# V projection of a hybrid decoder layer: the seventh chunk of its first pass formed by seven block products instead of eight

## The chip, the cores and the metric

One core of one Trainium2 chip runs the whole layer. The metric is device time in microseconds (us). A difference of 0.2% of this kernel's time, 2.2 us, is about what a measurement of it can tell from no change.

## The reference

One decoder layer for 256 tokens, 2048 features wide, in float32. One projection gives queries, keys and values of two groups of eight heads; differential attention in one group, block-sparse attention in the other; an output projection; layer norm; a gated feed-forward with a short convolution; layer norm again. What the change touches is the value columns of the first line below:

```
proj = h @ w_in[l]
v_d = proj[..., 2048:3072]        # 1024 value columns, differential heads
v_m = proj[..., 5120:6144]        # 1024 value columns, block-sparse heads
a_out = diff_attention(q_d, k_d, v_d, ...)
b_out = moba_attention(q_m, k_m, v_m, ...)
mix = concatenate([a_out, b_out]) @ w_out[l]
```

## The kernel before, in words

**Products.** Every float32 operand is split into a rounded part `hi` and a rest `lo` that TensorE (PE) takes in its faster format, and a product of two operands is three matmuls: hi·hi, hi·lo, lo·hi. ScalarE (ACT) writes `hi` by a copy, VectorE (DVE) writes `lo` as a difference.

**V projection.** It stands first in the program, as 16 chunks of the weight stream (`stream`, lines 80 to 84), numbered 0 to 15 here and in the code's `i`. Chunks 0 to 7 are the first pass and give value columns 0 to 1023, chunks 8 to 15 the second pass, columns 1024 to 2047. A chunk is 256 rows by 1024 columns of the weight, four blocks of 128x512. The step of a chunk (`run_v`, line 961) adds its share to four PSUM banks: bank 0 to 3 for token half t and column half c, as `CB[t][c]`, so that c = 1 is banks 1 and 3. An ordinary step is 24 matmuls of 128x512 (`mm_pair`), c = 0 first, then c = 1. Both passes use the same four banks, so the second pass may start on a bank only when ACT has copied the first pass's result out of it (`v_copy`): c = 0 in the middle of step 7, c = 1 at the beginning of step 8.

**Steps by seven products.** Chunks 9, 12 and 15 (`SEVEN`, line 51) go by a Strassen-like form: seven products of sums of blocks, 21 matmuls (`mm_seven`, line 737). Its operands are four sums of activation blocks (`act_sums`, DVE; `act_sums_split`, ACT and DVE), four sums of weight blocks and three raw weight blocks. They lie in the tiles `vhi` and `vlo` of seven blocks: places 0 to 2 are the raw blocks, 3 to 6 the sums. The tiles exist once, so a chunk's parts can be written only when the chunk by seven before it is done. `blocks_raw` (line 647) writes the raw blocks' hi by ACT, their lo by a negated ACT copy and an accumulating DMA on GpSimd's queue (POOL), and the first two sums; `blocks_lo`, `blocks_sum` and `blocks_hi` do the other two sums one after the other, since each is made from the one before, in the same buffer. Four of the seven products need partner sums that go to banks 4 to 7 (`MB`), which are added to the four results once, at the end (`v_shared`).

**What sets the order.** Each engine works its instructions in program order, and the code writes that order by hand. `begin(i)`, at the head of step i, prepares chunk i + 2 (`split`, or `blocks_raw` for one by seven) and issues the load of chunk i + 6; `middle(i)`, halfway in step i's matmuls, prepares half of chunk i + 3, or the sums of chunk i + 2 when that goes by seven. `at(step, fn)` hangs work on a begin or a middle; `urgent` runs it first there, `pending` last. Raw weights lie in four tiles used in turn, so chunk i + 4 loads into chunk i's tile once that is split; loads queue on SyncE (SP). In the first pass a chunk's share of the activations x is split as well (`split_x`).

Of the kernel before, what the change touches and what calls it, by code (L numbers as in the profile page):

```python
# [13 lines left out]
AF = mybir.ActivationFunctionType  # L14
ALU = mybir.AluOpType
# [28 lines left out]
VP = KT // 2  # L44
# [3 lines left out]

PART = 5

SEVEN = {"v": ((), range(1, 8, 3)), "d": ((), ()), "o": ((5,), (3,))}

ORDER = {"v": (1, 0, 2, 3), "d": (0, 1, 2, 3), "o": (2, 0, 1, 3)}

# [5 lines left out]
def hymba_layer(ctx: ExitStack, tc: tile.TileContext, a: dict):  # L60
    nc = tc.nc
    PE, DVE, ACT, POOL, SP = nc.tensor, nc.vector, nc.scalar, nc.gpsimd, nc.sync
# [15 lines left out]
    loaded, parts, waiting = {}, {}, {}  # L78

    stream = []  # L80
# [26 lines left out]
    def pieces(i, half=None):  # L107

        cuts = [0, 2048] if half is None and stream[i][0] != "v" else [0, 1024, 2048]
        both = [(x, y) for x, y in zip(cuts, cuts[1:])]  # L110
        return [p for p in both if half is None or p[0] // 1024 == half]

    def rows_of(p, x, y):
        return 2 * p + x // 512, 2 * p + y // 512
# [42 lines left out]
    def by_dma(i, half):  # L157

        kind, h, _, _ = stream[i]
        return kind == "k" and h < NDIFF and half == 1  # L160

    def split(i, half, both=None):

        if i >= NS or (i, half) in parts:
            return
        t = loaded[i] if half == 0 else loaded.pop(i)
        if both is None:
            o = MOVE_AT if stream[i][0] in "vod" or i - first_u in (0, 1) else 0
            hi, lo = (splits.tile([P, 1088], F32R, name=n)[:, o:o + 1024] for n in ("hi", "lo"))
        else:  # L170
            hi, lo = both[:, half], both[:, 2 + half]
        for x, y in pieces(i, half):
            if stream[i][0] == "v" and stream[i][2] == half == 0:
                split_x(*rows_of(stream[i][1], x, y))
            s = slice(x - 1024 * half, y - 1024 * half)
            if by_dma(i, half):
                ACT.activation(lo[:, s], t[:, x:y], AF.Copy, scale=-1.0)
                POOL.dma_start(lo[:, s], t[:, x:y], accum_op=ALU.add)
            ACT.activation(hi[:, s], t[:, x:y], AF.Copy)  # L179
            if not by_dma(i, half):  # L180
                DVE.tensor_tensor(lo[:, s], t[:, x:y], hi[:, s].bitcast(F32), ALU.subtract)  # L181
        parts[i, half] = (hi, lo)
# [45 lines left out]
    def split_x(k0, k1):  # L228
        t = xraw[:, k0 * S:k1 * S].rearrange("p (k t) -> p k t", t=S)
        ACT.activation(xh[:, k0:k1], t, AF.Copy)  # L230
        DVE.tensor_tensor(xl[:, k0:k1], t, xh[:, k0:k1].bitcast(F32), ALU.subtract)
# [83 lines left out]
    vals = keep.tile([P, 4, 2, 512], F32, name="val", tag="big")  # L315
# [5 lines left out]
    def at(step, fn, *args, rank=LATER):  # L321
        after.setdefault(step, []).append((rank, len(after.get(step, ())), fn, args))
# [224 lines left out]
    def down_slot():  # L547

        if "slot" not in kept:
            kept["slot"] = keep.tile([P, 16, 512], F32R, name="slot", tag="t2")  # L550
        return kept["slot"]
# [22 lines left out]
    aparts, sums = {}, {}  # L574
    sevens = [p for kind, p, n, j in stream if (kind, n) == ("d", 1) and j in SEVEN["d"][1]]

    def seven(i):
        kind, p, n, j = stream[i]
        if kind == "o":
            return n in SEVEN["o"][p]  # L580
        return kind in SEVEN and (j if kind == "d" else p) in SEVEN[kind][n] and (kind, n) != ("d", 0)

# [64 lines left out]
    def blocks_raw(i):  # L647

        kind, p, n, _ = stream[i]
        t = loaded[i].rearrange("p (b c) -> p b c", c=512)  # L650
        if kind == "d":
            slot = down_slot()
            hi, lo = slot[:, 0:7], slot[:, 7:14]
        elif kind == "o":
            if "oslot" not in kept:
                kept["oslot"] = keep.tile([P, 16, 512], F32R, name="oslot", tag="t2")
            hi, lo = kept["oslot"][:, 0:7], kept["oslot"][:, 7:14]
        else:
            lo = keep.tile([P, 7, 512], F32R, name="vlo", tag="ma")
            hi = keep.tile([P, 7, 512], F32R, name="vhi", tag="mb")  # L660
        b11, _, b22, b12 = ORDER[kind]
        f = [work.tile([P, 512], F32, name="tf", tag="m1") for _ in range(2)]
        blocks[i] = (hi, lo, f)
        if kind in "vo":
            ACT.activation(lo[:, 0:3], t[:, 0:3], AF.Copy, scale=-1.0)
            POOL.dma_start(lo[:, 0:3], t[:, 0:3], accum_op=ALU.add)
        DVE.tensor_tensor(f[0], t[:, b11], t[:, b12], ALU.subtract)
        DVE.tensor_tensor(f[1], t[:, b12], t[:, b22], ALU.add)
        for j in range(2):
            ACT.activation(hi[:, 3 + j], f[j], AF.Copy)  # L670
        if kind in "vo":
            ACT.activation(hi[:, 0:3], t[:, 0:3], AF.Copy)

    def blocks_lo(i, *js):
# [3 lines left out]

    def blocks_whole(i):

        if stream[i][0] == "d":
            hi, lo, _ = blocks[i]
            t = raws_of.pop(i).rearrange("p (b c) -> p b c", c=512)
            ACT.activation(hi[:, 0:3], t[:, 0:3], AF.Copy)
            DVE.tensor_tensor(lo[:, 0:3], t[:, 0:3], hi[:, 0:3].bitcast(F32), ALU.subtract)
# [12 lines left out]
    def blocks_hi(i, j):  # L698
        hi, _, f = blocks[i]
        ACT.activation(hi[:, 5 + j], f[0], AF.Copy)  # L700


    CB = ((bank[0], bank[1]), (bank[2], bank[3]))
    MB = {1: bank[4], 5: bank[5], 6: bank[6], 7: bank[7]}
# [154 lines left out]
    for kind, pairs in (("v", VP), ("d", PT)):  # L859
        for n in range(2):  # L860
            np_ = pairs - (PAIRED_END + 3 * PART if kind == "d" and n == 1 else 0)
            n7 = 2 * PART if kind == "d" and n == 0 else len(SEVEN[kind][n])
            if kind == "d" and n == 0:
# [14 lines left out]
    for n in range(2):  # L878
        for m in MO[n]:
            total["o", n, m] = 3 * len(SEVEN["o"][n])  # L880
        for t in range(2):
# [15 lines left out]
    def begin(i):  # L897

        urgent(i)
        j = i + 2  # L900
        if j < NS and seven(j):
            blocks_raw(j)
            act_sums(j)
        elif j - 1 < NS and seven(j - 1):
            blocks_sum(j - 1, 1)
            split(j, 1)
            blocks_hi(j - 1, 1)
            blocks_lo(j - 1, 3)
            blocks_whole(j - 1)
        else:  # L910
            split(j, 0)
            split(j, 1)
        if i >= first_d:
            act_back(i + 3)
        load(i + 6)
        pending(i)

    def middle(i):

        urgent(i + 0.5)  # L920
        if i + 2 < NS and seven(i + 2):
            blocks_lo(i + 2, 0)
            blocks_sum(i + 2, 0)
            blocks_lo(i + 2, 1)
            act_sums_split(i + 2)
            blocks_hi(i + 2, 0)
            split(i + 3, 0)
            blocks_lo(i + 2, 2)
        elif i + 3 < NS and not seven(i + 3):
            split(i + 3, 0)  # L930
        pending(i + 0.5)
# [14 lines left out]
    def value(n, t, c):  # L946
        return vals[:, 2 * n + c, t]

    def v_shared(n):
# [4 lines left out]
        for t, c, m in ((0, 1, 5), (1, 1, 5), (0, 0, 0), (None, None, 6), (0, 1, 0), (None, None, 7), (1, 0, 0), (1, 1, 0)):  # L954
            dst = u if t is None else v[t, c]
            DVE.tensor_tensor(dst, dst, MB[m] if m else u, ALU.add)

    def v_copy(n, t, c):
        ACT.activation(value(n, t, c), CB[t][c], AF.Copy)

    def run_v(i):
        _, p, n, _ = stream[i]
        for k in range(2):
            aparts[i, k] = xh[:, 2 * p + k], xl[:, 2 * p + k]
        if i == first_q - 1:
            v_copy(1, 1, 1)
            mm_seven(i, {m: lambda tc=tc: v_copy(1, *tc) for m, tc in ((2, (0, 0)), (3, (0, 1)), (4, (1, 0)))})
            at(i + 1, v_shared, 1)
        elif seven(i):
            mm_seven(i)  # L970
        elif i < 2:
            for k in range(2):
                if k == 1:
                    middle(i)
                for c in range(2):
                    mm_pair(i, c, k)
            done(i)
        else:
            for c in range(2):
                if c == 1:  # L980
                    if i == VP - 1:
                        for t in range(2):
                            v_copy(0, t, 0)
                    middle(i)
                for k in range(2):
                    mm_pair(i, c, k)
            done(i)
        if i == VP - 1:
            for t in range(2):
                at(i + 1, v_copy, 0, t, 1, rank=0)  # L990
        for k in range(2):
            aparts.pop((i, k))

# [78 lines left out]
    for i in range(first_o, last[0]):  # L1072
# [16 lines left out]
        n, j = stream[i][1:3]  # L1089
        if j == SEVEN["o"][n][-1]:  # L1090
            for part in range(2):
# [412 lines left out]
    for i in range(first_d, NS - PAIRED_END):  # L1504
        begin(i)
        _, p, n, j = stream[i]
# [201 lines left out]
```

## Time and profile before

| | before |
|---|---|
| median of 3 runs | 1109.13 us (1107.89 to 1109.57) |
| the profiled execution | 1107.91 us |
| its span, first to last instruction | 1106.1 us |
| PE busy | 1096.3 us |
| DVE busy | 923.2 us |
| ACT busy | 710.4 us |

A timeline row of the profile gives start, duration, engine, line, operation, tiles and count, and in brackets the idle time of the engine before it and what ended that. Matmuls overlap: a row's duration is longer than the distance of their starts, so a step's length is read from where the next step starts. The profiled execution took 1.22 us less than the median, within the spread of the runs.

### The profile page before, as it was taken

To read this page: it belongs to the slowest core of one execution; us is meant where nothing else is said; L and a number is where in the kernel's file an instruction comes from. 1 tells how busy PE (TensorE), PEld (TensorE's weight loads), DVE (VectorE), ACT (ScalarE), POOL (GpSimd) and SP (SyncE) were. 2 spreads that over 40 slices of the span, in tenths; PEclk is the share of its full clock that TensorE was granted. 3 is DMA by queue.
4 is the path that set the end of the run, shared out by engine and by line. 5 is a ranking of instruction groups with operands and counts; after the bars stand their busy time and mean duration, and the time that the engine had idled before them with its cause. 6 is when DMAs were issued, how large, how long until landed. Compare 5 with 4: busy or idle time off the path is not lost.

```text
span 1106.1 us, 16042 instructions
## 1 busy us (share of the span) xinstructions
PE 1096.3 (99%) x5893; PEld 945.4 (85%) x5893; DVE 923.2 (83%) x1561; ACT 710.4 (64%) x1146; POOL 68.0 (6%) x96
## 2 busy tenths in 40 slices
PE   9999999999999999999999999999999999999997
PEld 7888888888888898888888888888888888888886
DVE  6776778888778878888899989889988899988785
ACT  6765676654555386666666676667767676666742
POOL 0000110000000000000000000000000010000103
PEclk9999999999999999999999999999999999999999
DMA  9898776444466646888888888898988888889862
GB/s 333 284 287 282 243 230 210 153 153 153 169 204 217 227 152 222 288 275 276 269 308 278 282 285 295 300 331 272 327 295 271 268 297 285 272 286 297 280 223 77
DMA packets 63471, 280.90 MB, mean 254 GB/s; under 512 B 6481, under 2 KB 7969, under 8 KB 45601
## 3 DMA queue, kind: packets, MB, share of 16 engines
q1 hardware_dynamic: 53024, 235.05, 57.4%
q0 software_dynamic: 10224, 44.57, 17.9%
q8 instruction: 46, 0.75, 0.3%
q10 hardware_dynamic: 144, 0.26, 0.1%
q14 instruction: 33, 0.26, 0.1%
HBM read 233.17 MB, written 20.45 MB: 229 GB/s over the span
## 4 chain that ended last, share of the span: by engine, by line
PE 94%; DMA 2%; DVE 2%; ACT 1%; issue 0%; SPq 0%; DVEq 0%; POOL 0%; ACTq 0%
PE bank L279 94%; DMA ring<-in_w_d 1%; DMA rslot<-ring 1%; PE bank L425 0%; DMA raw<-in_w_v 0%; DVE z L1104 0%; DVE st L496 0%; PE bank L1113 0%; PE bank L472 0%; DVE z L493 0%; ACT rslot L1370 0%; DVE h L1128 0%; DVE rslot L1470 0%; ACT tslot L825 0%; DVE lo L198 0%
## 5 line engine op out<-in xcount | busy, mean ns | idle before, releaser
L279 PE MATMUL bank<-h,hi 128*128 128x512 f32 x1376 | 481.0, 390 | 0.4 <-ACT ub L1233 0.4
L279 PE MATMUL bank<-h,lo 128*128 128x256 f32 x1376 | 387.9, 282 | 0.0
L279 PEld LDWEIGHTS bank<-h,hi 128*128 128x128 f32 x1376 | 258.2, 188 | 55.4 <-ACT ub L1233 0.8
L279 PEld LDWEIGHTS bank<-h,lo 128*128 128x128 f32 x1376 | 259.9, 189 | 3.6
L198 DVE TENSOR_TENSOR lo<-raw,hi 128x1024 fp32r<-128x1024 f32 x171 | 208.0, 1220 | 16.7 <-ACT hi L190 16.6
L181 DVE TENSOR_TENSOR lo<-raw,hi 128x1024 fp32r<-128x1024 f32 x123 | 147.6, 1221 | 52.6 <-ACT hi L179 48.4
L279 PE MATMUL bank<-x,hi 128*128 128x512 f32 x512 | 182.9, 398 | 0.0
L190 ACT ACTIVATE hi<-raw 128x1024 fp32r<-128x1024 f32 x171 | 178.5, 1048 | 0.0
L179 ACT ACTIVATE hi<-raw 128x1024 fp32r<-128x1024 f32 x131 | 136.6, 1056 | 60.7 <-PE bank L279 32.7
L279 PE MATMUL bank<-x,lo 128*128 128x256 f32 x512 | 144.2, 282 | 0.0
L825 ACT ACTIVATE tslot<-tf 128x512 fp32r<-128x512 f32 x140 | 86.2, 627 | 61.1 <-DVE tf L1414 24.4
L279 PEld LDWEIGHTS bank<-x,hi 128*128 128x128 f32 x512 | 96.2, 188 | 20.6 <-issue 1.0
L828 DVE TENSOR_TENSOR tslot<-tf,tslot 128x512 fp32r<-128x512 f32 x140 | 94.9, 688 | 11.1 <-ACT tslot L825 10.4
L1233 ACT ACTIVATE ub<-bank 128x512 f32<-128x512 f32 x86 | 50.8, 591 | 80.5 <-PE bank L279 80.5
L279 PEld LDWEIGHTS bank<-x,lo 128*128 128x128 f32 x512 | 96.8, 189 | 0.2
L279 PE MATMUL bank<-hi,x 128*128 128x512 f32 x208 | 55.9, 391 | 0.3 <-ACT hi L210 0.3
L1242 DVE TENSOR_TENSOR ub<-ub 128x256 f32<-128x256 f32 x86 | 36.2, 421 | 17.6 <-ACT ub L1233 17.5
L1371 POOL DMA_DIRECT2D rslot<-ring x18 | 15.8, 880 | 503.2 <-ACT sp L831 454.2
L279 PEld LDWEIGHTS bank<-hi,x 128*128 128x128 f32 x208 | 39.0, 188 | 8.9 <-ACT hi L210 0.7
L279 PE MATMUL bank<-tslot,more 128*128 128x512 f32 x180 | 46.0, 391 | 0.0
L279 PE MATMUL bank<-tslot,sp 128*128 128x512 f32 x180 | 45.2, 391 | 0.0
L559 ACT ACTIVATE gc<-ub,vec 128x256 f32<-128x256 f32 x43 | 25.6, 595 | 22.1 <-DVE ub L1242 22.1
(267 smaller groups left out, 1604.0 us busy)
## 6 DMA issues: line engine op xcount, KB each, us to landing
raw<-in_w_u SPq DMA_DIRECT2D x88, 1024.0 KB, 7.3
raw<-in_w_qk SPq DMA_DIRECT2D x32, 1024.0 KB, 5.0
raw<-in_w_d SPq DMA_DIRECT2D x52, 512.0 KB, 5.2
ring<-in_w_d SPq DMA_DIRECT2D x36, 512.0 KB, 9.1
raw<-in_w_o SPq DMA_DIRECT2D x16, 1024.0 KB, 4.9
raw<-in_w_v SPq DMA_DIRECT2D x28, 512.0 KB, 8.5
rslot<-ring POOLq DMA_DIRECT2D x18, 768.0 KB, 7.0
dparts<-rslot SPq DMA_DIRECT2D x20, 512.0 KB, 8.4
```

Source lines behind the costliest of these rows:

```text
L179: ACT.activation(hi[:, s], t[:, x:y], AF.Copy)
L181: DVE.tensor_tensor(lo[:, s], t[:, x:y], hi[:, s].bitcast(F32), ALU.subtract)
L190: ACT.activation(hi, t[:, half * 1024:half * 1024 + 1024], AF.Copy)
L198: DVE.tensor_tensor(lo, t[:, half * 1024:half * 1024 + 1024], hi.bitcast(F32), ALU.subtract)
L279: PE.matmul(out, lhsT, rhs, start=start, stop=stop)
L559: ACT.activation(gates[f], g, AF.Identity, bias=vec[:, C_CB + f:C_CB + f + 1], scale=vec[:, C_W + 2 * FT + f:C_W + 2 * FT + f + 1])
L825: ACT.activation(side["t"][:, 0, j], f, AF.Copy)
L828: DVE.tensor_tensor(side["t"][:, 1, j], f, side["t"][:, 0, j].bitcast(F32), ALU.subtract)
L1233: ACT.activation(t.rearrange("p j t -> p (j t)"), up_bank(i), AF.Copy)
L1242: DVE.tensor_tensor(u[:, 0], u[:, 0], u[:, 1], ALU.add)
L1371: POOL.dma_start(side["r"][:, 1], w[:, 0:3], accum_op=ALU.add)
```

## The change

Chunk 6, the last but one of the first pass, goes by seven products. With that: 

- Its share of x is split at the head of `blocks_raw`, its raw blocks' hi and lo are written last (`blocks_whole`: a copy by ACT, a difference by DVE of 128x1536 each) and not by the accumulating DMA, and the splits of chunk 7 move from the middle of step 4 and the begin of step 5 to behind all that.
- A new `v_products` in the middle of step 7 takes the shared products of the first pass out of banks 4 to 7: one ACT copy and four DVE additions, into the second pass's place in `vals`. `v_sum`, two and a half steps later, adds them to the first pass's results.
- For the second pass's chunks by seven (9, 12, 15) the ACT copy of the raw blocks' hi (128x1536) moves from `blocks_raw` to `blocks_hi` in the middle of the step.

```
-SEVEN = {"v": ((), range(1, 8, 3)), "d": ((), ()), "o": ((5,), (3,))}
+SEVEN = {"v": ((6,), range(1, 8, 3)), "d": ((), ()), "o": ((5,), (3,))}
...
+        if kind == "v" and n == 0:
+            split_x(2 * p, 2 * p + 2)
+        added = kind == "o" or (kind, n) == ("v", 1)
...
-        if kind in "vo":
+        if added:
             ACT.activation(lo[:, 0:3], t[:, 0:3], AF.Copy, scale=-1.0)
             POOL.dma_start(lo[:, 0:3], t[:, 0:3], accum_op=ALU.add)
...
-        if kind in "vo":
+        if kind == "o":
             ACT.activation(hi[:, 0:3], t[:, 0:3], AF.Copy)
...
-        if stream[i][0] == "d":
+        if stream[i][0] == "d" or (stream[i][0], stream[i][2]) == ("v", 0):
...
         ACT.activation(hi[:, 5 + j], f[0], AF.Copy)
+        if j == 0 and stream[i][0] == "v" and stream[i][2] == 1:
+            ACT.activation(hi[:, 0:3], loaded[i].rearrange("p (b c) -> p b c", c=512)[:, 0:3], AF.Copy)
...
             blocks_sum(j - 1, 1)
-            split(j, 1)
+            if j - 1 >= VP:
+                split(j, 1)
             blocks_hi(j - 1, 1)
             blocks_lo(j - 1, 3)
             blocks_whole(j - 1)
+            if j - 1 < VP:
+                split(j, 0)
+                split(j, 1)
...
-            split(i + 3, 0)
+            if i + 2 >= VP:
+                split(i + 3, 0)
...
+    def v_products():
+
+        w = {(t, c): value(1, t, c) for t in range(2) for c in range(2)}
+        ACT.activation(w[0, 0], MB[1], AF.Copy)
+        for dst, m, src in (((1, 1), 6, (0, 0)), ((0, 1), 5, (1, 1)), ((1, 0), 7, (1, 1)), ((1, 1), 5, (1, 0))):
+            DVE.tensor_tensor(w[dst], MB[m], w[src], ALU.add)
+
+    def v_sum():
+        DVE.tensor_tensor(vals[:, 0:2], vals[:, 0:2], vals[:, 2:4], ALU.add)
...
+    at(VP - 0.5, v_products, rank=0)
...
+            at(i + 2.5, v_sum)
```

The order on ACT around the middle of step 7 and the begin of step 8, before: `vlo` and `vhi` are chunk 9's parts, `tf` its block sums, bank_71 to bank_74 are banks 0 to 3, the `L179` row is the first half of chunk 10.

```order
L665 ACTIVATE vlo<-raw 128x1536
L670 ACTIVATE vhi<-tf 128x512 x2
L672 ACTIVATE vhi<-raw 128x1536
L959 ACTIVATE val<-bank_71 128x512
L959 ACTIVATE val<-bank_73 128x512
L639 ACTIVATE e<-vf 128x256
L639 ACTIVATE wh<-vf 128x256
L700 ACTIVATE vhi<-tf 128x512
L179 ACTIVATE hi<-raw 128x1024
L959 ACTIVATE val<-bank_72 128x512
L959 ACTIVATE val<-bank_74 128x512
```

The same place on ACT after the change, where bank_75 is bank 4, the first of the shared products:

```order
L673 ACTIVATE vhi<-tf 128x512 x2
L979 ACTIVATE val<-bank_71 128x512
L979 ACTIVATE val<-bank_73 128x512
L971 ACTIVATE val<-bank_75 128x512
L639 ACTIVATE e<-vf 128x256
L639 ACTIVATE wh<-vf 128x256
L703 ACTIVATE vhi<-tf 128x512
L705 ACTIVATE vhi<-raw 128x1536
L179 ACTIVATE hi<-raw 128x1024
L979 ACTIVATE val<-bank_72 128x512
L979 ACTIVATE val<-bank_74 128x512
```

The copy of bank 4 is new, and the 128x1536 copy went from ahead of the copies of banks 0 and 2 to ahead of those of banks 1 and 3.

The order on DVE from chunk 6's split to the first sum of chunk 9, before: `x` and `z` are the activations, the first `L181` row the two `lo` of chunk 6, the second those of chunks 7 and 8.

```order
L231 TENSOR_TENSOR x_79<-z,x_79 128x2x256
L181 TENSOR_TENSOR lo<-raw,hi 128x1024 x2
L231 TENSOR_TENSOR x_79<-z,x_79 128x2x256
L181 TENSOR_TENSOR lo<-raw,hi 128x1024 x4
L667 TENSOR_TENSOR tf<-raw 128x512
```

The end of the stretch that stands there now on DVE, from the first `lo` of chunk 6's sums to chunk 7's and 8's `lo`:

```order
L680 TENSOR_TENSOR vlo<-tf,vhi 128x512
L697 TENSOR_TENSOR tf<-raw,tf 128x512
L680 TENSOR_TENSOR vlo<-tf,vhi 128x512
L640 TENSOR_TENSOR e<-vf,e 128x256
L640 TENSOR_TENSOR wl<-vf,wh 128x256
L680 TENSOR_TENSOR vlo<-tf,vhi 128x512
L697 TENSOR_TENSOR tf<-raw,tf 128x512
L680 TENSOR_TENSOR vlo<-tf,vhi 128x512
L688 TENSOR_TENSOR vlo<-raw,vhi 128x1536
L231 TENSOR_TENSOR x_79<-z,x_79 128x2x256
L181 TENSOR_TENSOR lo<-raw,hi 128x1024 x4
```

The two `lo` of 128x1024 that chunk 6 had became fifteen operations (the last ten of them stand here, up to `L688`), and chunk 7 stands behind them.

Chunk 9's first parts on DVE, after the change, where bank_76 to bank_78 are banks 5 to 7:

```order
L670 TENSOR_TENSOR tf<-raw 128x512
L671 TENSOR_TENSOR tf<-raw 128x512
L619 TENSOR_TENSOR vf<-z 128x128
L620 TENSOR_TENSOR vf<-z 128x128
L621 TENSOR_TENSOR vf<-vf,z 128x128
L622 TENSOR_TENSOR vf<-z,vf 128x128
L973 TENSOR_TENSOR val<-bank_77,val 128x512
L973 TENSOR_TENSOR val<-bank_76,val 128x512
L973 TENSOR_TENSOR val<-bank_78,val 128x512
L973 TENSOR_TENSOR val<-bank_76,val 128x512
L680 TENSOR_TENSOR vlo<-tf,vhi 128x512
L697 TENSOR_TENSOR tf<-raw,tf 128x512
```

The four additions from the banks came in between the activation sums (`vf`) and the first `lo` of chunk 9's sums; the rows around them stood next to each other before.

## The prediction

> **What bounds the kernel now.** First the page: the busy times, and the chain that ended last.
>
> ```profile
> PE 1096.3 (99%) x5893; PEld 945.4 (85%) x5893; DVE 923.2 (83%) x1561; ACT 710.4 (64%) x1146; POOL 68.0 (6%) x96
> PE 94%; DMA 2%; DVE 2%; ACT 1%; issue 0%; SPq 0%; DVEq 0%; POOL 0%; ACTq 0%
> ```
>
> PE is hardly ever idle, so a matmul less is time saved, provided that its operands and its banks are ready. Whether they are is read where the change works. The table of stretches, cut at the starts of steps 6, 7, 8 and 9 (start and end, length, then busy time and count of PE, PEld, DVE, ACT, POOL, and the granted clock):
>
> ```profile
> 38.16:43.60 5.44, 5.44 (x26) 4.50 (x24) 4.50 (x9) 4.81 (x5) 1.62 (x4) 1.00 0.91 312
> 43.60:49.04 5.44, 5.44 (x26) 4.51 (x24) 1.58 (x4) 2.75 (x6) 0.00 (x0) 1.00 0.98 241
> 49.04:54.48 5.44, 5.44 (x26) 4.50 (x24) 4.96 (x6) 4.75 (x7) 0.00 (x0) 1.00 0.29 76
> 54.48:59.24 4.76, 4.76 (x23) 3.94 (x21) 3.77 (x8) 0.16 (x2) 0.00 (x0) 1.00 0.97 303
> ```
>
> The weight loads count the matmuls: 24 take 5.44 us, and the 21 of step 9, by seven, 4.76 us, so 0.227 us each. DVE is idle for most of step 7 (1.58 of 5.44 us) and busy in the steps around it.
>
> Then the timelines of ACT and DVE, which feed PE: how far ahead of it are they? ACT, from chunk 6's second half; then from chunk 8's last split to chunk 10's:
>
> ```profile
> 30.37 1.06 ACT L179 ACTIVATE hi<-raw 128x1024 fp32r<-128x1024 f32 x1 [0.22 <-DMA raw<-in_w_v]
> ...
> 37.91 1.06 ACT L179 ACTIVATE hi<-raw 128x1024 fp32r<-128x1024 f32 x1 [1.66 <-PE bank L279]
> 38.87 1.47 ACT L665 ACTIVATE vlo<-raw 128x1536 fp32r<-128x1536 f32 x1
> 40.86 1.24 ACT L670 ACTIVATE vhi<-tf 128x512 fp32r<-128x512 f32 x2 [0.51 <-DVE tf L667]
> 42.00 1.48 ACT L672 ACTIVATE vhi<-raw 128x1536 fp32r<-128x1536 f32 x1
> 46.29 1.09 ACT L959 ACTIVATE val<-bank 128x512 f32<-128x512 f32 x2 [2.81 <-PE bank L279]
> 47.26 0.42 ACT L639 ACTIVATE e<-vf 128x256 fp32r<-128x256 f32 x1
> 47.57 0.42 ACT L639 ACTIVATE wh<-vf 128x256 fp32r<-128x256 f32 x1
> 47.88 0.63 ACT L700 ACTIVATE vhi<-tf 128x512 fp32r<-128x512 f32 x1
> 48.40 1.05 ACT L179 ACTIVATE hi<-raw 128x1024 fp32r<-128x1024 f32 x1
> 49.35 1.08 ACT L959 ACTIVATE val<-bank 128x512 f32<-128x512 f32 x2
> 50.30 1.08 ACT L179 ACTIVATE hi<-raw 128x1024 fp32r<-128x1024 f32 x1
> ```
>
> Read the last but one: banks 1 and 3 are copied out by 50.43. Step 8 writes bank 1 after its twelve matmuls on banks 0 and 2, at 49.04 + 12 x 0.227 = 51.76. So this copy has 1.3 us in hand, and it stands behind everything above it on ACT. DVE, with chunk 9's sums from 40.14 on:
>
> ```profile
> 29.37 0.68 DVE L231 TENSOR_TENSOR x<-z,x 128x512 fp32r<-128x512 f32 x1
> ...
> 40.14 0.68 DVE L667 TENSOR_TENSOR tf<-raw 128x512 f32<-128x512 f32 x1
> 40.74 0.69 DVE L668 TENSOR_TENSOR tf<-raw 128x512 f32<-128x512 f32 x1
> 41.34 0.28 DVE L619 TENSOR_TENSOR vf<-z 128x128 f32<-128x128 f32 x1
> ...
> 42.40 0.69 DVE L677 TENSOR_TENSOR vlo<-tf,vhi 128x512 fp32r<-128x512 f32 x1
> 43.12 0.69 DVE L694 TENSOR_TENSOR tf<-raw,tf 128x512 f32<-128x512 f32 x1
> 43.73 0.68 DVE L677 TENSOR_TENSOR vlo<-tf,vhi 128x512 fp32r<-128x512 f32 x1
> 47.71 0.43 DVE L640 TENSOR_TENSOR e<-vf,e 128x256 fp32r<-128x256 f32 x1 [3.30 <-ACT e L639]
> 48.06 0.42 DVE L640 TENSOR_TENSOR wl<-vf,wh 128x256 fp32r<-128x256 f32 x1
> ...
> 53.70 2.36 DVE L181 TENSOR_TENSOR lo<-raw,hi 128x1024 fp32r<-128x1024 f32 x2
> ...
> ```
>
> Starts on DVE are 0.6 us apart for 128x512 (0.72 where one uses the result before it), 1.06 for the four activation sums, 0.35 for 128x256, 1.13 for 128x1024.
>
> **The change part by part.** All times are on this execution's clock.
>
> *Removed: three matmuls.* 24 - 21 = 3, at 0.227: -0.68 us, if chunk 6's parts are ready. Step 6 is then 38.16 to 42.92, step 8 begins at 48.36 and wants bank 1 at 51.08, bank 3 at 51.31.
>
> *Added on DVE: chunk 6's parts.* Its first sum needs both halves; the second landed for the ACT row at 30.37, so it starts at 30.4. By the spacings above: two sums 31.6, activation sums 32.7, lo 33.4, sum 34.0, lo 34.6, two of 128x256 35.3, lo 36.0, last sum done at 36.7. ACT copies it (36.7 to 37.3) and then the raw blocks (1.48, to 38.7); DVE writes their lo, 128x1536. No DVE row of before has that size; by 0.69 for 512 and 1.22 for 1024 it is 1.76 us (estimate; bounds 1.22 and 1.91), to 40.5. Step 6 reads it in its fifth product, at 38.16 + 13 x 0.227 = 41.1. Ready by 0.6 us: no stall, though with no more than that in hand. Chunk 7's x and four halves follow, 0.6 + 4 x 1.13: DVE is free at 45.6. Chunk 7 is needed from 43.8 and has its first lo at 42.2: no stall. Chunk 9's first sum, at 40.14 before, thus begins at 45.6, 5.4 us later, while PE is 0.7 us earlier.
>
> *Moved and added: what follows in step 7.* From 45.6 the chain passes between DVE and ACT. Sum 46.3; ACT's two hi copies (0.63 + 0.53) 47.4; the copies of banks 0 and 2 (1.08) 48.5, wanted at 48.36, which costs 0.1; the new copy of bank 4, 49.1. DVE's four additions use each other's results; the group of the same kind in the second pass has
>
> ```profile
> L956 DVE TENSOR_TENSOR val<-val,bank 128x512 f32<-128x512 f32 x2 | 1.3, 680 | 0.0
> ```
>
> so about 0.7 each, 2.8, to 51.9. Behind them stand chunk 9's first lo and third sum, done at 53.2 (0.72 + 0.69). ACT waits for it with the third hi copy (53.8), then the moved 128x1536 copy (1.48, less 0.1 of overlap: 55.2), chunk 10's half (0.95: 56.1), and only then the copies of bank 1 (56.7) and bank 3 (57.3).
>
> PE is queued behind them: it has banks 1 and 3 to write at 51.08 and 51.31, and every later matmul stands behind that on its engine. Stall: 57.3 - 51.3 = 6.0 us, with the 0.1 before. Bounds: each DVE spacing is from a row, so the ends are 5.0 (the raw lo at its lower bound, the additions at 0.6) and 6.6 (upper bound, additions at 0.78).
>
> *Next late, if these copies were early.* Chunk 9's last sum: its third and fourth lo stand behind chunk 10's halves on DVE, done at 58.0 and 60.4 by the same walk; step 9 would begin at 53.80 and read the last at 53.80 + 10 x 0.227 = 56.1: a stall of 4.3. After the stall of 6.0 step 9 begins at 59.8 and reads it at 62.1: hidden.
>
> *Loads and queues.* Raw tiles come free later: chunk 10 loads when chunk 6's raw lo is done, 40.5 and not about 32. SP's order is unchanged. The view of DMA issues up to 125 us:
>
> ```profile
> raw<-in_w_v SPq DMA_DIRECT2D x28, 512.0 KB, 8.5
> vlo<-raw POOLq DMA_DIRECT2D x3, 768.0 KB, 9.7
> ```
>
> Chunk 10 lands by 49.0 and is split at 55: free. Chunk 9's accumulating DMA starts at 44.7 (its ACT copy waits for step 6's end, 42.9, + 1.47 + 0.3), lands at 54.4 and is read at 56.7 at the earliest: free. `v_sum`, 2048 wide, falls in step 9 when PE is 6 us later; I take 0, at most its own 2.3 (by size).
>
> *The clock.* PE's idle gap is about 5.4 us long. [...]
>
> ```profile
> 1.19 3.17 PE L279 MATMUL bank<-idle 128*128 128x512 bf16 x7 [1.19 <-DVE idle L886]
> 1099.07 0.73 PE L279 MATMUL bank<-rows,side 6*128 6x512 f32 x2 [0.36 <-ACT side L1624]
> 1103.40:1106.10 2.70, 0.00 (x0) 0.00 (x0) 0.00 (x0) 0.00 (x0) 0.00 (x0) 0.50 0.23 80
> ```
>
> After the last matmul (to 1099.8) the granted clock is 0.50 from 1103.4, so within 3.6 us of idle time; at the start seven matmuls lie about 0.43 us apart, until some 4.4 us. After the gap PE would then run at half pace for up to 3.2 us, losing 1.5. Ends 0 and 1.5; I take 1.1, nearer the upper, since the gap is longer than 3.6.
>
> [...]
>
> *Sum.* -0.7 + 6.0 + 1.1 = +6.4 us: 1107.9 + 6.4 = 1114.3 for the profiled execution. The median of the runs lies 1.2 above it: 1109.1 + 6.4 = 1115.5.
>
> **The rivals.**
>
> - *Full forecast, with the clock falling:* 1115.5, within 1114.8 to 1117.
> [...]
> - *The copies in time, step 9's parts late:* if ACT did not wait for the third sum. -0.7 + 4.3: 1112.7. Against it: the order puts that copy ahead.
> - *Not slower: it does what it says.* The 0.7 saved stands alone: 1108.4. The place is the copy of bank 1: it must end by 51.1, so chunk 9's third sum would have to be done by about 47.6 and not 53.2. For it speaks DVE's idle time in step 7; against it, that fifteen operations of chunk 6 come just before and the four additions just in it.
> - *More is late:* step 6 stops for its raw lo, or a load slips, 2 to 3 us on top: 1118.
>
> **How the numbers follow.** Full forecast 0.45, stall without the clock 0.30, step 9 alone 0.08, not slower 0.12, more 0.05. The forecast of both stalls has its own range of 1113.4 to 1117; with step 9's rival below and part of the last above, 1112.5 to 1117.8 holds eight in ten. 0.2% is 2.2 us, about what a measurement can tell from no change; the saving alone, 0.7, is less, so "not slower" falls within it, with 0.13 for it and small stalls. Faster by more would take a gain of three times what is removed: 0.02. Slower: 0.85.
>
> **What would show it.** In the changed kernel's trace: step 6 by seven starting at 38.2 with no gap; PE idle from about 51.2 to 57, put down to ACT's copy of `val`; on ACT the third `vhi` copy near 53.3, waiting for DVE's sum; the clock below 1 after the gap. Wrong would be: no gap in step 8 (the walk on DVE is too slow), a gap in step 6 or 9 (other parts are late), or a gap of less than 4 us.

## The result and the profile after

| | before | after |
|---|---|---|
| median of 6 runs each, one chip | 1108.76 us (1107.89 to 1109.57) | 1114.72 us (1113.26 to 1116.03) |
| profiled execution | 1107.91 us | 1114.46 us |
| span | 1106.1 us | 1112.7 us |

The ratio is 1.0054 (95% interval 1.0044 to 1.0064): slower by 0.54%, 6.0 us.

The page's busy times and chain hardly differ from those of before:

```profile
PE 1098.7 (99%) x5890; PEld 945.9 (85%) x5890; DVE 933.8 (84%) x1579; ACT 713.6 (64%) x1152; POOL 68.4 (6%) x96
PE 90%; DMA 4%; DVE 3%; ACT 1%; issue 1%; DVEq 0%; SPq 0%; POOL 0%; ACTq 0%
```

Three matmuls fewer, and yet 2.4 us more of PE busy, mostly because some of them run at half pace (clock 0.50 for 3.42 us). The table of stretches, cut at the starts of steps 6, 7, 8 and 9, then at the edges at which the granted clock changed (56.71 and 60.13) and at two such lengths before (columns as before: start and end, length, busy time and count of PE, PEld, DVE, ACT, POOL, then the clock):

```profile
38.50:43.26 4.76, 4.76 (x22) 3.94 (x21) 4.76 (x5) 4.09 (x6) 0.00 (x0) 1.00 0.45 153
43.26:48.70 5.44, 5.44 (x25) 4.50 (x24) 4.27 (x9) 4.26 (x7) 1.88 (x4) 1.00 0.93 338
48.70:60.84 12.14, 7.58 (x25) 5.58 (x24) 10.26 (x15) 7.83 (x11) 0.00 (x0) 0.86 0.61 144
49.88:53.30 3.42, 1.70 (x8) 1.08 (x6) 3.35 (x7) 0.65 (x2) 0.00 (x0) 1.00 1.03 252
53.30:56.71 3.41, 0.57 (x2) 0.27 (x2) 1.67 (x3) 3.41 (x5) 0.00 (x0) 1.00 0.41 85
56.71:60.13 3.42, 3.42 (x8) 2.68 (x9) 3.38 (x6) 2.72 (x4) 0.00 (x0) 0.50 0.24 61
```

Step 6 has its 21 matmuls in 4.76 us and no gap: 5.44 - 4.76 = 0.68 us are saved. Step 8 takes 12.14 us in place of 5.44, though PE is busy in 7.58 of them. From 56.71 to 60.13 the clock is half. PE's timeline shows where the step stops:

```profile
50.97 0.61 PE L279 MATMUL bank<-lo,x 128*128 128x512 f32 x2
56.14 2.08 PE L279 MATMUL bank<-hi,x 128*128 128x512 f32 x4 [4.56 <-ACT val L979]
...
60.84 0.39 PE L279 MATMUL bank<-vhi,e 128*128 128x512 f32 x1
```

After the twelve matmuls on banks 0 and 2 the next would have started at 51.42; it starts at 56.14, released by ACT's copy of `val`, which frees bank 1. The second bank costs some 0.26 more. ACT's timeline, from chunk 9's first `hi` copies to the copies of banks 1 and 3 (L979; L971 is bank 4's, L703 the third `hi`, L705 the moved raw one):

```profile
45.91 1.16 ACT L673 ACTIVATE vhi<-tf 128x512 fp32r<-128x512 f32 x2 [1.18 <-DVE tf L670]
46.97 1.07 ACT L979 ACTIVATE val<-bank 128x512 f32<-128x512 f32 x2
47.93 0.60 ACT L971 ACTIVATE val<-bank 128x512 f32<-128x512 f32 x1
...
52.65 0.63 ACT L703 ACTIVATE vhi<-tf 128x512 fp32r<-128x512 f32 x1 [3.52 <-DVE tf L697]
53.19 1.47 ACT L705 ACTIVATE vhi<-raw 128x1536 fp32r<-128x1536 f32 x1
54.56 1.04 ACT L179 ACTIVATE hi<-raw 128x1024 fp32r<-128x1024 f32 x1
55.51 1.06 ACT L979 ACTIVATE val<-bank 128x512 f32<-128x512 f32 x2
```

ACT stands idle for 3.52 us ahead of the third `hi` copy, with the copies that PE wants queued three places behind it. It waits for DVE (L670 first sum of a chunk, L688 chunk 6's raw `lo`, L973 the additions, L680 a `lo`, L697 the third sum):

```profile
29.93 0.69 DVE L670 TENSOR_TENSOR tf<-raw 128x512 f32<-128x512 f32 x1 [0.32 <-DMA raw<-in_w_v]
...
38.29 1.76 DVE L688 TENSOR_TENSOR vlo<-raw,vhi 128x1536 fp32r<-128x1536 f32 x1 [0.69 <-ACT vhi L687]
...
45.11 0.69 DVE L670 TENSOR_TENSOR tf<-raw 128x512 f32<-128x512 f32 x1
...
48.55 2.74 DVE L973 TENSOR_TENSOR val<-bank,val 128x512 f32<-128x512 f32 x4 [1.10 <-ACT val L971]
51.21 0.68 DVE L680 TENSOR_TENSOR vlo<-tf,vhi 128x512 fp32r<-128x512 f32 x1
51.93 0.69 DVE L697 TENSOR_TENSOR tf<-raw,tf 128x512 f32<-128x512 f32 x1
```

So the path runs through two engines in turn: DVE's first sum of chunk 9 (45.11, after chunk 6's and 7's parts), ACT's copies, bank 4's last among them, DVE's four additions, its third sum, ACT's `hi` copies, the banks.

The account up to step 9, which starts at 60.84 and started at 54.48, 6.36 us earlier: step 6 begins 0.34 later than before (38.50 against 38.16; PE's first matmul of step 0 already came at 5.36 and not 4.71, where nothing of the change stands in any queue), -0.68 saved, +4.72 for the gap, +0.26 for the second bank, and +1.7 for 3.42 us at half clock: +6.34. (The last twelve matmuls of step 8 take 4.70 us in place of 2.72; the 0.26 is what the clock leaves of that.) The rest of the 6.6 in the span comes later.

### The profile page after: what moved, and what is told of

The parts are those of the page before. It is cut to its first block, busy times and chain, and to the rows that moved or that the text cites. A ratio compares the mean times of both kernels' runs of the same rounds, so it can differ in the third digit from the quotient of the medians.

```text
span 1112.7 us, 16059 instructions
## 1 busy us (share of the span) xinstructions
PE 1098.7 (99%) x5890; PEld 945.9 (85%) x5890; DVE 933.8 (84%) x1579; ACT 713.6 (64%) x1152; POOL 68.4 (6%) x96
## 4 chain that ended last, share of the span: by engine, by line
PE 90%; DMA 4%; DVE 3%; ACT 1%; issue 1%; DVEq 0%; SPq 0%; POOL 0%; ACTq 0%
PE bank L279 89%; DMA raw<-in_w_v 2%; DMA ring<-in_w_d 1%; DMA z<-in_xT 1%; DMA rslot<-ring 1%; PE bank L425 0%; DVE lo L181 0%; DVE val L973 0%; DVE vlo L680 0%; DVE tf L697 0%; DVE z L1127 0%; DVE st L496 0%; PE bank L1136 0%; PE bank L472 0%; DVE z L493 0%
## 5 line engine op out<-in xcount | busy, mean ns | idle before, releaser
L181 DVE TENSOR_TENSOR lo<-raw,hi 128x1024 fp32r<-128x1024 f32 x121 | 144.9, 1221 | 50.3 <-ACT hi L179 48.7
L179 ACT ACTIVATE hi<-raw 128x1024 fp32r<-128x1024 f32 x129 | 134.2, 1055 | 55.4 <-PE bank L279 30.9
L279 PE MATMUL bank<-hi,x 128*128 128x512 f32 x192 | 53.2, 399 | 4.6 <-ACT val L979 4.6
L279 PEld LDWEIGHTS bank<-hi,x 128*128 128x128 f32 x192 | 36.7, 193 | 13.9 <-ACT val L979 5.3
```

The source lines that it names most:

```text
L279: PE.matmul(out, lhsT, rhs, start=start, stop=stop)
```

## The experiments

The theory: the copies of banks 1 and 3 are late, because on ACT they stand behind chunk 9's third `hi` copy, which waits for DVE's third sum, which stands behind chunk 6's parts and the four additions; and behind the idle gap PE's clock is lower (0.50 from 56.71 to 60.13). Rivals: the moved raw copy alone does it; step 9's parts do; the clock adds nothing. Differences are against runs of the kernel before on the same chip at the same time.

**The moved raw copy alone** (chunk 6 by eight products again):

```
-SEVEN = {"v": ((6,), range(1, 8, 3)), ...
+SEVEN = {"v": ((), range(1, 8, 3)), ...
-    at(VP - 0.5, v_products, rank=0)
-            at(i + 2.5, v_sum)
```

> Only the move of the raw blocks' hi copy in the second pass is left; chunk 6 goes by eight products as before. Theory (what is late is chunk 9's third sum on DVE; the moved copy only rides on it): the copies of banks 1 and 3 end at about 51.8 us, just when step 8 wants them, so 0 to +0.3 us against the kernel before and no idle gap over 0.3 us in step 8. Rival (the moved copy, 1.48 us ahead of the copies of banks 1 and 3, is what costs): a gap of 1 us or more in step 8 and +1 us or more.

Measured: 1108.43 us against 1108.42, ratio 1.0001 (0.9992 to 1.0009). ACT's timeline there:

```profile
48.90 1.48 ACT L705 ACTIVATE vhi<-raw 128x1536 fp32r<-128x1536 f32 x1
...
51.22 1.08 ACT L979 ACTIVATE val<-bank 128x512 f32<-128x512 f32 x2
```

The move pushes the copies of banks 1 and 3 to 51.22, and this uses up what they had in hand without a gap on PE. Alone it costs nothing.

**Without the additions** (and without `v_sum`, which adds what they make):

```
-        for dst, m, src in (((1, 1), 6, (0, 0)), ...):
-            DVE.tensor_tensor(w[dst], MB[m], w[src], ALU.add)
-            at(i + 2.5, v_sum)
```

> The changed kernel without the four additions out of banks 5 to 7 and without the later sum: the shared products of the first pass are left out of its values. Theory (the additions and the wait for the copy of bank 4 delay chunk 9's third sum by 3.7 us, chunk 6's parts by 5): the idle gap in step 8 shrinks from 4.7 to about 2 us, the granted clock stays at 1.00 after it, and the time is about +1.8 us against before. Rival (ACT's own queue, the moved copy and chunk 10's half, sets the copies): the gap stays over 4 us and the time at +6. Second rival (the additions are everything): no gap, -0.7.

Measured: 1108.32 us against 1108.42, ratio 1.0001 (0.9992 to 1.0010): less than expected. PE's and ACT's rows at the place,

```profile
52.16 1.45 PE L279 MATMUL bank<-hi,x 128*128 128x512 f32 x4 [0.40 <-ACT val L977]
```

```profile
51.51 1.08 ACT L977 ACTIVATE val<-bank 128x512 f32<-128x512 f32 x2
```

and DVE's first sum of chunk 9:

```profile
44.76 0.69 DVE L670 TENSOR_TENSOR tf<-raw 128x512 f32<-128x512 f32 x1
```

The copies start at 51.51, 4.0 us earlier than in the changed kernel (55.51), and PE loses some 0.9 us only, most of which the saved 0.68 pays. From chunk 9's first sum to the copies it is 6.75 us here and 10.40 in the changed kernel (45.11 to 55.51): the additions and their wait are worth 3.65, as expected (3.7). By that the gap of 4.7 should have come down to 1.0 and not to the 2 expected; it came to 0.6, since the chain starts 0.35 earlier here (44.76 against 45.11) and PE reaches step 8 0.2 later. The stall thus takes chunk 6's parts and the additions together; the parts alone push it to the brink. The trace shows this, and not the time alone: `v_sum` is left out as well, and it costs time in a kernel without the stall, as the last runs show.

**The copies of banks 1 and 3 ahead of the third `hi` copy** (in the begin of step 8 the third sum's work goes behind them):

```
             act_sums_split(i + 2)
-            blocks_hi(i + 2, 0)
-            if i + 2 >= VP:
-                split(i + 3, 0)
-            blocks_lo(i + 2, 2)
+            if i + 1 != VP:
+                third(i + 2)
...
+            if i == VP:
+                third(j - 1)
             blocks_sum(j - 1, 1)
```

> The changed kernel with the copies of banks 1 and 3 ahead, on ACT, of chunk 9's third hi copy, its raw hi copy and chunk 10's half. [...] Rival (the order of the copies is all that is late): no gap at all, -0.7.

Measured: 1111.51 us against 1108.42, ratio 1.0031 (1.0020 to 1.0043). Step 8 has no gap; step 9 has three, on PE's timeline, and the stretches show the clock:

```profile
57.27 0.50 PE L279 MATMUL bank<-vlo,wh 128*128 128x512 f32 x1 [1.45 <-DVE vlo L680]
...
58.66 0.49 PE L279 MATMUL bank<-vhi,x 128*128 128x512 f32 x1 [0.66 <-ACT vhi L703]
59.74 0.50 PE L279 MATMUL bank<-vlo,x 128*128 128x512 f32 x1 [0.58 <-DVE vlo L680]
```

```profile
56.96:60.37 3.41, 1.86 (x6) 1.03 (x7) 3.38 (x5) 2.39 (x3) 0.00 (x0) 1.00 0.37 107
60.37:63.79 3.42, 3.42 (x10) 2.65 (x9) 3.42 (x3) 0.14 (x1) 0.00 (x0) 0.50 0.90 290
```

The order on ACT is shown to make the gap of step 8, and the next late thing is what the prediction named: chunk 9's last parts. The sizes came out smaller than the prediction's walk for it: +3.1 us and not -0.7 + 4.3 = +3.6, and three waits of 3.3 us together (1.6, 0.8 and 0.8, from where the next matmul would have started) and not 4.3. In this profile the clock is 0.50 for 3.42 us from 60.37, behind three waits of which the longest is 1.6 us. For the other five executions the runs give the mean granted clock alone: 0.997 to 0.998, against 0.996 in the profiled one and 0.997 to 0.999 in the kernel before beside it.

**The gap filled** with 18 matmuls of zeros into bank 4, which is free then:

```
                             v_copy(0, t, 0)
                     middle(i)
+                    if i == VP:
+                        for _ in range(18):
+                            mm(bank[4], idle[:, 0:P], idle, True, True)
```

> The changed kernel with eighteen matmuls of zeros into bank 4 between the two halves of step 8, 3.9 us of work where PE stood idle. Theory (1.7 us of the loss is the halved clock after the gap): the granted clock stays at 1.00 there, the copies of banks 1 and 3 end where they did, and the time is 1.3 to 1.7 us below the changed kernel's, so +4.3 to +4.7 against before. Rival (other engines are late by then, and the slow stretch hides behind them): the clock stays up, but the time is that of the changed kernel, +6.

Measured: 1111.63 us against 1108.42, ratio 1.0032 (1.0020 to 1.0043). PE's timeline, and the stretch of the gap:

```profile
51.88 4.06 PE L279 MATMUL bank<-idle 128*128 128x512 bf16 x17
56.24 1.45 PE L279 MATMUL bank<-hi,x 128*128 128x512 f32 x4 [0.31 <-ACT val L979]
```

```profile
51.50:56.20 4.70, 4.38 (x20) 1.79 (x19) 2.92 (x6) 3.44 (x5) 0.00 (x0) 1.00 0.76 160
```

Bank 1 comes free as late as in the changed kernel (56.24 against 56.14), but the clock stays at 1.00 (so it does from 56.20 to 60.00), and by the medians the kernel is some 3 us faster than the changed one (+3.2 against the kernel before, in place of +6.0), more than the 1.3 to 1.7 expected. The traces show a part of that: from the release of bank 1 to the start of step 9 it is 3.12 us here (56.24 to 59.36) and 4.70 in the changed kernel (56.14 to 60.84), so 1.6 for the clock. A second profile of the changed kernel shows that more can be lost, 2.2 by the same measure. The rest of the 3 us is not placed; the profiled execution here was the slowest of its six, 0.9 above their median.

**The changed kernel once more**, beside the next three:

> [...]

Measured: 1114.76 us against 1108.06, ratio 1.0060 (1.0048 to 1.0073). This is +6.7, a little more than the +6.0 of the first comparison. Its stretches, cut where the clock changed (53.76 and 60.59), halfway between, and as much before:

```profile
50.35:53.76 3.41, 1.18 (x6) 0.64 (x4) 2.49 (x5) 2.12 (x3) 0.00 (x0) 1.00 0.71 144
53.76:57.18 3.42, 2.06 (x5) 1.57 (x6) 2.53 (x4) 2.74 (x4) 0.00 (x0) 0.50 0.02 5
57.18:60.59 3.41, 3.41 (x10) 2.64 (x9) 3.41 (x4) 2.52 (x3) 0.00 (x0) 0.50 0.58 177
```

Behind the same stall the clock is half for 6.83 us here, twice the 3.42 of the first profile. DVE's first sum of chunk 9, ACT's copies of banks 1 and 3 and PE's next matmul:

```profile
44.09 0.68 DVE L670 TENSOR_TENSOR tf<-raw 128x512 f32<-128x512 f32 x1
```

```profile
54.49 1.06 ACT L979 ACTIVATE val<-bank 128x512 f32<-128x512 f32 x2
```

```profile
55.12 2.14 PE L279 MATMUL bank<-hi,x 128*128 128x512 f32 x4 [3.59 <-ACT val L979]
```

The whole chain runs 1.0 us earlier than in the first profile, and is as long: 10.40 us from the sum to the copies in both. The gap is shorter (PE resumes at 55.12, 3.75 us late) and the matmuls are slow for longer: from 55.12 to 60.59, 5.47 us at half pace, which loses 2.7. The sum, 6.4, is close to the first profile's 4.72 + 0.26 + 1.7 = 6.7.

**The raw copy back in its old place** (chunk 6 by seven, additions and all):

```
-        if kind == "o":
+        if added:
             ACT.activation(hi[:, 0:3], t[:, 0:3], AF.Copy)
...
-        if j == 0 and stream[i][0] == "v" and stream[i][2] == 1:
-            ACT.activation(hi[:, 0:3], loaded[i]...
```

> The changed kernel with the raw blocks' hi copy back in its old place, ahead of the copies of banks 0 and 2. Theory (ACT loses the same 1.48 us, only earlier, and everything behind waits for the same third sum): two gaps, about 1.2 us at the start of step 8 and 4 us in its middle, PE going on at the same time as in the changed kernel, so +5 to +6.5 against before. Rival (the moved copy is the cost): the gap in the middle falls below 3.5 us and the time to about +4.

Measured: 1113.70 us against 1108.06, ratio 1.0048 (1.0036 to 1.0061). DVE, ACT and PE:

```profile
43.98 0.68 DVE L670 TENSOR_TENSOR tf<-raw 128x512 f32<-128x512 f32 x1
...
48.92 2.74 DVE L971 TENSOR_TENSOR val<-bank,val 128x512 f32<-128x512 f32 x4 [2.59 <-ACT val L969]
```

```profile
53.02 0.63 ACT L703 ACTIVATE vhi<-tf 128x512 fp32r<-128x512 f32 x1 [3.52 <-DVE tf L697]
...
54.50 1.06 ACT L977 ACTIVATE val<-bank 128x512 f32<-128x512 f32 x2
```

```profile
55.13 2.13 PE L279 MATMUL bank<-hi,x 128*128 128x512 f32 x4 [3.26 <-ACT val L977]
```

From chunk 9's first sum to the copies it is 10.52 us (43.98 to 54.50), about as long as in the changed kernel (10.40 in both profiles), and PE goes on at 55.13 against 55.12 in the second of them. So the place of the raw copy costs nothing within the stall either, as the theory had it: behind the third `hi` copy it delays the copies of banks 1 and 3 by its own length, and ahead of the copies of banks 0 and 2 it delays bank 4's, so that DVE waits 2.59 us for that and not 1.10. The gap at the start of step 8 that was expected did not come, and the one in the middle, 3.4 us long since PE reaches it only at 51.7, lies just under the rival's 3.5; the time is the theory's. The kernel is still 1.1 us faster than the changed one beside it. In the profiles that is the clock: it is half for 3.42 us here (54.68 to 58.10) and for 6.83 there, and from the release of bank 1 to step 9 it is 4.25 us (to 59.38) in place of 5.35. That the place of the copy is the reason is not shown.

**Another order around step 8**: the four additions ahead of the middle of step 7, chunk 9's `hi` copies of its first sums behind the copies of banks 0 and 2, the third sum's work behind those of banks 1 and 3, chunk 10's halves behind chunk 9's parts:

```
+        if i != VP + 1:
+            first_hi(i)
...
+    def first_hi(i):
+        hi, _, f = blocks[i]
         for j in range(2):
             ACT.activation(hi[:, 3 + j], f[j], AF.Copy)
...
+            if i == VP:
+                act_sums_split(j - 1)
+                blocks_hi(j - 1, 0)
+                blocks_lo(j - 1, 2)
             blocks_sum(j - 1, 1)
-            if j - 1 >= VP:
+            if j - 1 >= VP and i != VP:
                 split(j, 1)
...
-            if j - 1 < VP:
+            if j - 1 < VP or i == VP:
...
+            if i + 1 == VP:
+                first_hi(i + 2)
...
+            if i + 1 == VP:
+                pending(i + 0.5)
+                return
...
-    at(VP - 0.5, v_products, rank=0)
+    at(VP - 1, v_products, rank=0)
```

> The changed kernel in another order, with the same work: the shared products are taken out before chunk 9's first sums (ACT's copy of bank 4 at the begin of step 7), ACT copies banks 0 and 2 before chunk 9's first hi copies and banks 1 and 3 before its activation sums, and chunk 10's halves go behind all of chunk 9's parts. Theory (no engine lacks time for chunk 6, the order does): no gap in steps 6 to 9, clock 1.00; but the later sum of 128x2048 on DVE (2.3 us) pushes chunk 12's parts, with gaps of about 2 us together in step 12; +1.0 to +1.6 us against before. Rival (DVE lacks the time for chunk 6's parts in any order): gaps of 3 us or more in steps 8 and 9, +3 us or more.

Measured: 1110.07 us against 1108.06, ratio 1.0019 (1.0010 to 1.0028): +2.0, somewhat more than the +1.0 to +1.6 expected. In the profile there is no gap in steps 6 to 9 and the clock stays full there, as the theory had it; but the gaps it put in step 12 are not there either. The loss sits 45 us after the change, in the q/k phase. PE's timeline there, and two pieces of the chain of waits that leads to it:

```profile
101.03 0.39 PE L279 MATMUL bank<-x,lo 128*128 128x256 f32 x1 [1.54 <-DMA lo<-raw]
```

```profile
59.30 2.20 DVE val L990
...
88.61 12.38 DMA lo<-raw
```

The accumulating DMA that writes the first `lo` of the q/k weights was issued at 88.61 and took 12.38 us; in the kernel before it was issued at 86.29 and took 11.0. On the chain to it stands `v_sum` (L990 here).

**The same with `v_sum` on GpSimd**:

```
-        DVE.tensor_tensor(vals[:, 0:2], vals[:, 0:2], vals[:, 2:4], ALU.add)
+        POOL.tensor_tensor(vals[:, 0:2], vals[:, 0:2], vals[:, 2:4], ALU.add)
```

> The kernel above with the later sum of 128x2048 moved from DVE to GpSimd, which is idle there. Theory (that sum alone is late in step 12): no gap over 0.3 us in any step of the projection; -0.7 us against before, the three matmuls. Rival (GpSimd's sum slows DVE or holds back the accumulating DMA of chunk 12 on its queue): gaps in step 12, 0 to +3 us.

Measured: 1112.42 us against 1108.06, ratio 1.0037 (1.0023 to 1.0051): +4.4, so the expectation fell, and the loss is more than the rival's 0 to +3. GpSimd's and DVE's timelines:

```profile
50.47 5.12 POOL L990 TENSOR_TENSOR val<-val 128x2048 f32<-128x2048 f32 x1 [3.28 <-DVE vlo L685]
```

```profile
50.44 0.69 DVE L702 TENSOR_TENSOR tf<-raw,tf 128x512 f32<-128x512 f32 x1
51.05 5.10 DVE L685 TENSOR_TENSOR vlo<-tf,vhi 128x512 fp32r<-128x512 f32 x1
```

A difference on DVE that takes 0.68 us elsewhere takes 5.10 beside the sum on GpSimd, and PE waits 1.3 us for what stands behind it, and 1.6 for the accumulating DMA of the q/k phase. The work was taken from DVE and DVE lost more than the work.

**The changed kernel, and the other order, each without `v_sum`**:

```
-            at(i + 2.5, v_sum)
```

> The changed kernel with VectorE's sum over two pairs of buffers (128x2048, 2.29 us in the changed kernel's trace) left out, so that two of the results lack one of their terms; the four additions and everything else stay. The prediction put this sum at nothing in the changed kernel. Theory A: it is hidden behind the wait in step 8, after which PE is behind by more than it takes; the time stays within 0.3 us of the changed kernel's, 1114.4 to 1115.1, and the wait in step 8 and the half clock behind it are there as before. Theory B: the sum is felt where the first weights of the q/k phase come late (waits of 0.28 and 0.85 us at 105 in the two traces of the changed kernel, put down to the accumulating DMA); then 0.3 to 0.9 us less, 1113.9 to 1114.4, and that wait gone.

Measured: 1114.35 us against 1108.21, ratio 1.0054 (1.0040 to 1.0068): +6.1, as with the sum (+6.0 and +6.7). The time by itself decides nothing: it lies at the edge between the two theories. The trace does: the wait in step 8 is there (3.7 us), and so is the wait in the q/k phase, 0.90 us here and 0.46 in the second profile of the changed kernel. On PE's timeline:

```profile
105.70 0.38 PE L279 MATMUL bank<-x,lo 128*128 128x256 f32 x1 [0.90 <-DMA lo<-raw]
```

> The reordered kernel (e5_reordered, 1110.07) with the same sum left out, so that two of the results lack one of their terms. There PE is not behind, and the accumulating DMA of the q/k phase was issued 2.3 us later than in the kernel before (88.61 against 86.29), about the sum's 2.2 us, and took 1.4 us longer. Theory A: the sum pushed VectorE's later work and with it that issue; without it the issue comes at about 86.4, PE's wait of 1.93 us at 99 goes, and the time falls by 1.5 to 1.9 us to 1108.2 to 1108.6, level with the kernel before. Theory B: the wait comes from the DMA's longer flight alone; then half of it or more stays and the time is 1109.2 or above.

Measured: 1107.77 us against 1108.21, ratio 0.9994 (0.9986 to 1.0003). This is less than the 1108.2 to 1108.6 expected. The wait ahead of 101.03 is gone and the time with it. GpSimd's queue:

```profile
87.42 0.86 POOL L178 DMA_DIRECT2D lo<-raw  x1 [9.90 <-ACT lo L177]
```

The DMA is issued 1.2 us earlier than with the sum, not the whole 2.2; it landed 2.3 us earlier, so the other 1.1 came from its shorter flight (11.3 for 12.4). The size agrees with the sum as the cause; of the flight it is not shown why it changed.

**The sum in two halves**, each put where DVE waited for ACT, in the middles of steps 10 and 13; nothing is left out:

```
-            at(i + 2.5, v_sum)
...
+            if i in (VP + 2, VP + 5):
+                v_sum((i - VP) // 3)
...
-    def v_sum():
-        DVE.tensor_tensor(vals[:, 0:2], vals[:, 0:2], vals[:, 2:4], ALU.add)
+    def v_sum(c):
+        DVE.tensor_tensor(vals[:, c], vals[:, c], vals[:, 2 + c], ALU.add)
```

> The reordered kernel with the sum cut into two halves of 128x1024, and each put where VectorE stood idle for 1.75 us waiting for ScalarE's copy of a chunk's part (ends of that wait at 66.91 and 82.00 in the trace of e8_reordered_no_sum). Nothing is left out of the computation. A half is worked out at about 1.2 us, from 2.28 for the whole. Theory: each half fits in its wait, the accumulating DMA of the q/k phase is issued within 0.3 us of the kernel without the sum, and the time is that of e8_reordered_no_sum, 1107.5 to 1108.2, at or a little under the kernel before. [...]

Measured: 1108.21 us against 1108.30, ratio 0.9998 (0.9989 to 1.0007). DVE's timeline around the two halves (L992):

```profile
64.99 1.22 DVE L992 TENSOR_TENSOR val<-val 128x1024 f32<-128x1024 f32 x1
66.82 1.23 DVE L181 TENSOR_TENSOR lo<-raw,hi 128x1024 fp32r<-128x1024 f32 x1 [0.62 <-ACT hi L179]
...
80.08 1.22 DVE L992 TENSOR_TENSOR val<-val 128x1024 f32<-128x1024 f32 x1
81.91 1.22 DVE L181 TENSOR_TENSOR lo<-raw,hi 128x1024 fp32r<-128x1024 f32 x1 [0.61 <-ACT hi L179]
```

Each half fits in its wait and some 0.6 us of it is left, and PE waits nowhere up to the q/k phase, as the theory had it. Seven products in chunk 6 can be had without a loss, some 6 us below the changed kernel; a gain over the kernel before is not shown, and with 0.68 us to be had at most it is smaller than a measurement can tell.

## Why the prediction came out as it did

The forecast was +6.4, from three terms; the runs gave +6.0 (and +6.7 the second time). The mechanism and its place were right; the sizes of two terms were off in opposite directions, the stall too large by 1.0 in one profile and 2.2 in the other, the clock too small by 0.6 and 1.6, so that the total came this close is in part luck. The median of 1114.72 lies nearer the stall without the clock (1109.1 - 0.7 + 6.0 = 1114.4) than the forecast (1115.5), partly since the kernel before came out 0.4 us lower in six runs than in three; it is the traces that decide for the clock.

- *Three matmuls*: -0.68, as predicted, with step 6 free of gaps. DVE wrote the raw blocks' `lo` in the 1.76 us estimated, done at 40.05 where 40.5 was predicted.
- *The stall*: 6.0 predicted, 4.72 + 0.26 measured (3.75 in the second profile). The walk was right step for step, but it ran late: chunk 6's second half landed 0.44 us earlier than in the trace of before, so the first sum started at 29.93 and not 30.4, and chunk 9's at 45.11 and not 45.6; the copies ended at 56.57, not 57.3. PE itself came 0.34 later. These 0.7 and 0.3 are the difference. The walk took a load's landing from one execution as fixed; in the second profile of the changed kernel the whole chain ran another 1.0 us earlier.
- *Additions, moved copy*: 2.8 us for the additions, and the moved copy on the path. The additions took 2.74, and 3.65 with their wait; without them the stall all but goes, so it takes them and chunk 6's parts together. (The additions without chunk 6's parts are no kernel that was run.) The moved copy is on the path as the walk had it, but its move costs nothing: not by itself, and not within the stall, where in its old place it lengthens the path by as much ahead of bank 4's copy.
- *The clock*: 1.1 predicted with 1.5 as the upper end; 1.7 in one profile and 2.7 in the other; by the run with the gap filled 1.6 and 2.2, of a gain of some 3 in its median. This is the term that came out above its upper end. No run shows its length of 3.2 us: that was read off the seven matmuls at the start, 0.43 us apart, and the granted clock is 1.00 there (1.20 to 4.30). What the runs showed is half clock for 3.42 us (56.71 to 60.13) and for 6.83 (53.76 to 60.59), and PE was not idle throughout the 3.41 us before it: from 53.30 to 56.71 there were two matmuls, from 50.35 to 53.76 six. The chance of 0.30 for the stall without the clock was the author's estimate, and too high: the clock fell in both profiles of the changed kernel and in those with the raw copy back and without the sum (there matmuls are 0.43 us apart from 56.59 to 59.98), and the mean granted clock of all eleven executions of the changed kernel is 0.995 to 0.997, against 0.998 to 0.999 with the gap filled.
- *Next late*: step 9's last parts. Shown by the run with the copies first, at +3.1 where the rival gave -0.7 + 4.3 = 3.6, with waits of 3.3 us for the 4.3. That the order puts the third `hi` copy ahead was the right ground against it.
- *Loads and queues, `v_sum` at nothing*: held in the changed kernel as far as the runs can tell, where the sum lies behind the stall. The margin behind it is thin: in the kernel without the stall it cost 2.3 us, in another phase.

What stays open: why the accumulating DMA of the q/k phase takes between 7.0 us (issued at 87.32, with the halves) and 13.4 us (issued at 92.31, the changed kernel without the sum), and where the 1 us or so comes from by which filling the gap gains more in the medians than the traces show up to step 9.

## What to carry to other kernels

A saving on the busiest engine is worth what the engines that feed it have in hand at that place: walk their order from the last wait before the change to the result that PE needs next, and ask what stands ahead of it in the queue. Work that is hidden behind a wait (the sum) is paid for once the wait is taken away, and the loss may show far behind (2.3 us here, with the wait 45 us later). Moving a copy to another place on the same engine (the raw copy) need not help, since it delays what then stands behind it. Put added work where an engine already waits for another, and price an idle gap on PE with the half clock behind it (here 3.42 and 6.83 us at 0.50, behind gaps of 4.7 and 3.75 us).

## What the runs showed of the hardware

- Half clock lasted 3.42 us (the changed kernel, the copies first, the raw copy back) or 6.83 (the changed kernel's second profile). Matmuls in the 3.41 us before it, with PE's busy time: two in 0.57 (53.30 to 56.71), six in 1.18 (50.35 to 53.76), six in 1.86 (56.96 to 60.37, the copies first, no wait over 1.6 us), three in 0.60 (51.27 to 54.68, the raw copy back). Behind the eight in 1.70 from 49.88 to 53.30 the clock stayed at 1.00. What of this sets the clock was not tested.
- A DVE operation of 128x512 (`vlo<-tf,vhi`) took 5.10 us beside a GpSimd addition of 5.12 us, for 0.68 alone. It ended at 56.15, 0.56 after GpSimd's end at 55.59. Why it took so long is not shown.
- The accumulating DMA of 512 KB, the first of the q/k phase, took 11.0 us in the kernel before, 12.3 in the changed kernel, 12.4 in the other order, 11.3 in that without the sum and 7.0 with the halves.
